# Global branch's output product: which groups stand between the last value product and the last attention outputs

## The chip, the cores and the metric

The kernel runs on one core of one Trainium2 chip. The metric is the device time of one execution in microseconds; before the change the median of three runs is 1576.53 us (1576.3 to 1577.41).

## The reference

One layer of a diffusion backbone over 1024 latent tokens of 1024 channels, with 256 context tokens that serve as further keys. Two attention branches run on the same input, A windowed and B global. What bears on the change is how their outputs are merged:

```python
def _global_attention(q, k_all, v_all):
    ...
        p = jax.nn.softmax(_gqa_scores(q_blk, k_all), axis=-1)
        return _gqa_values(p, v_all)
...
def _merge_branches(o_a, o_b, gate_logits, w_branch_a, w_branch_b, w_out):
    g_a, g_b = jnp.split(jax.nn.sigmoid(gate_logits), 2, axis=-1)
    return (g_a * (o_a @ w_branch_a) + g_b * (o_b @ w_branch_b)) @ w_out
...
        y = _latent_token_mixer(h, kv_ctx, w_in[l], b_in[l], attn_sink[l], q_norm_g[l], k_norm_g[l],
                                w_branch_a[l], w_branch_b[l], w_out[l], rope)
        x = _layer_norm(DEEPNORM_ALPHA * x + gate1 * y, ln1_g[l], ln1_b[l])
        h = x * (1.0 + scale2) + shift2
        y = _conv_ffn(h, w_up[l], conv_w[l], conv_b[l], w_down[l])
```

The change is in `o_b @ w_branch_b` times its gate: a product of 512 by 1024 weights with the outputs of the global branch.

## The kernel before, in words

Everything lies transposed: channels on the 128 partitions, tokens along the row. A tile of 128 channels by 1024 tokens is a feature tile, and there are eight of them, f = 0 to 7. A product in full precision is made of three matmuls on a high and a low part of each operand (`mm3`, lines 88 to 91): high by high (L89), low part of the outputs (L90), low part of the weights (L91). A high part is a rounded copy (L81 on ScalarE, L83 on GpSimd), a low part the difference (L86).

The attention runs in units of one branch, 128 query tokens and four heads. Line 831 loops over the units; each round merges three lists of steps by their place on a common scale and calls them: scores of the present unit, the value product of the unit before (transposes `ptr` of the probabilities, L530; their high and low parts `pth` and `ptl`, L539 and L540; the product `av`, L551 and L552), and filler steps. After the last unit (u == nu) only the value steps of the last unit and fillers are left. Its output goes through a copy `avs` on ScalarE (L557), `up` on GpSimd (L559), a sum `ot` on VectorE (L562), a scaling on GpSimd (L565) and the split into `O` on GpSimd (L83, L86). The output tiles `O` of the second token half (hf = 1) are complete only then; those of the first half (hf = 0) have been complete since the first four blocks of 128 tokens.

The fillers of the end belong to the output product of the global branch (br = 1). A group of `branch_steps` (line 802) is one feature tile and one token half: it loads the stored gate into `bT`, runs twelve matmuls into a bank `b`, and multiplies the bank into `bT` on VectorE (L813). `first` holds the groups of feature tiles 0 and 1 in the order (0, hf 0), (0, hf 1), (1, hf 0), (1, hf 1), on banks of the attention's pool `ps2`. Behind the attention a new pool of banks, `ps3`, is opened: `big` tiles of 1024 tokens, three of them, and `sml` tiles of 512, two of them. There `wb` (line 947) makes the high and low weights of tiles 2 to 5, `merge` (line 938) adds the two branches' products (L940) and splits the sum into `mh` (ScalarE) and `ml` (VectorE) for the output projection `y`, and the loop at line 953 takes tiles 2 to 7, both token halves alternating.

The kernel's scheduler decides where the instructions of a step stand on each engine's queue; each engine then takes its queue in order. SyncE issues most loads (`sgd` into `bT` at L955, weights at L901, `z` at L935), also in the order of its queue.

## Time and profile before

| | |
|---|---|
| median of three runs | 1576.53 us |
| the profiled execution | 1576.9 us, of which the span is 1575.1 |
| mean granted clock of TensorE | 0.995 |
| TensorE busy | 1526.1 us (97%) |
| VectorE busy | 1194.1 us (76%) |
| ScalarE busy | 808.9 us (51%) |
| GpSimd busy | 759.1 us (48%) |
| last value product ends, first output projection starts | 778.73 us, 821.77 us |

Times in the trace are microseconds from the start of the span. A matmul of 128 by 512 is shown with 0.39 us though the next one starts after 0.23: matmuls overlap, and the distance of their starts is what they cost. In the windows view the clock column is the share of full speed that TensorE was granted. In the timeline the bracket is the engine's idle time before the instruction and what ended it.

### The profile page before, as it was taken

To read this page: it belongs to the slowest core of one execution; us is meant where nothing else is said; L and a number is where in the kernel's file an instruction comes from. 1 tells how busy PE (TensorE), PEld (TensorE's weight loads), DVE (VectorE), ACT (ScalarE), POOL (GpSimd) and SP (SyncE) were. 2 spreads that over 40 slices of the span, in tenths; PEclk is the share of its full clock that TensorE was granted. 3 is DMA by queue.
4 is the path that set the end of the run, shared out by engine and by line. 5 is a ranking of instruction groups with operands and counts; after the bars stand their busy time and mean duration, and the time that the engine had idled before them with its cause. 6 is when DMAs were issued, how large, how long until landed. Compare 5 with 4: busy or idle time off the path is not lost.

```text
span 1575.1 us, 21929 instructions
## 1 busy us (share of the span) xinstructions
PE 1526.1 (97%) x7614; PEld 1264.2 (80%) x7614; DVE 1194.1 (76%) x1761; ACT 808.9 (51%) x1439; POOL 759.1 (48%) x737
## 2 busy tenths in 40 slices
PE   6999999999999999999999999999999999999997
PEld 5878788878886888777778898888888888888886
DVE  7797545728888777788684779888888888656797
ACT  5422222448888667688522465444544444435533
POOL 0574212426666566555422644666667765021053
PEclk9999999999999999999999999999999999999999
DMA  9685663322237565533354132333334446997823
GB/s 376 225 303 185 221 206 102 114 79 79 58 88 177 114 142 127 115 82 71 111 174 98 54 108 81 120 108 107 108 107 107 108 107 171 353 274 225 260 93 108
DMA packets 112016, 230.25 MB, mean 146 GB/s; under 512 B 13505, under 2 KB 27329, under 8 KB 111809
## 3 DMA queue, kind: packets, MB, share of 16 engines
q1 hardware_dynamic: 96464, 199.20, 38.5%
q0 software_dynamic: 10400, 20.19, 8.4%
q10 hardware_dynamic: 5040, 9.46, 1.6%
q8 instruction: 60, 0.98, 0.3%
q14 instruction: 52, 0.42, 0.1%
HBM read 177.61 MB, written 65.87 MB: 155 GB/s over the span
## 4 chain that ended last, share of the span: by engine, by line
PE 81%; DVE 8%; DMA 3%; ACT 3%; issue 3%; POOL 1%; SPq 0%; DVEq 0%; ACTq 0%; POOLq 0%
PE ptr L530 5%; PE p L90 4%; PE p L91 4%; PE p L89 4%; PE b L89 3%; PE b L90 3%; PE b L91 3%; PE g L89 3%; PE g L90 3%; PE g L91 3%; PE s L413 2%; PE av L551 2%; PE a L91 2%; PE c L89 2%; PE d L91 2%
## 5 line engine op out<-in xcount | busy, mean ns | idle before, releaser
L540 DVE TENSOR_TENSOR ptl<-ptr,pth 128x512 fp32r<-128x512 f32 x188 | 124.7, 684 | 28.2 <-ACT pth L539 25.5
L539 ACT CAST pth<-ptr 128x512 fp32r<-128x512 f32 x188 | 106.5, 588 | 59.1 <-PE ptr L530 35.5
L86 DVE TENSOR_TENSOR ld<-rd,hd 128x1024 fp32r<-128x1024 f32 x77 | 97.7, 1284 | 48.2 <-ACT hd L81 41.6
L530 PE MATMUL ptr<-ident,p 128*128 128x128 f32 x816 | 126.3, 277 | 7.4 <-DVE ptl L540 5.1
L425 ACT ACTIVATE p<-p,nm 128x1024 f32<-128x1024 f32 (+2 forms) x128 | 125.3, 981 | 10.7 <-DVE p L458 10.0
L530 PEld LDWEIGHTS ptr<-ident,p 128*128 128x128 f32 x816 | 93.9, 140 | 36.8 <-DVE ptl L540 10.9
L81 ACT CAST hd<-rd 128x1024 fp32r<-128x1024 f32 x77 | 79.6, 1051 | 85.3 <-PE p L91 61.4
L551 PE MATMUL av<-pth,VT 128*128 128x512 f32 x236 | 104.7, 444 | 1.0 <-ACT avs L557 0.5
L89 PE MATMUL p<-hd 128*128 128x512 f32 x264 | 103.2, 391 | 0.0
L91 PE MATMUL p<-hd,ld 128*128 128x512 f32 x264 | 102.7, 389 | 0.0
L90 PE MATMUL p<-ld,hd 128*128 128x512 f32 x264 | 102.7, 389 | 0.0
L86 POOL TENSOR_TENSOR wlg<-wg,whg 128x512 fp32r<-128x512 f32 x32 | 46.0, 1445 | 112.1 <-ACT whg L81 111.9
L89 PE MATMUL g<-hh,whg 128*128 128x512 f32 x256 | 99.9, 390 | 0.0
L91 PE MATMUL g<-hh,wlg 128*128 128x512 f32 x256 | 99.6, 389 | 0.0
L90 PE MATMUL g<-hl,whg 128*128 128x512 f32 x256 | 99.6, 389 | 0.0
L552 PE MATMUL av<-ptl,VT 128*128 128x512 f32 x236 | 97.6, 413 | 1.6 <-POOL ptl L86 1.4
L458 DVE TENSOR_SCALAR_CACHE_REDUCE p<-s,cvt,nmc 128x1024 f32<-128x1024 f32 x64 | 84.4, 1339 | 11.7 <-PE s L414 11.1
L413 PE MATMUL s<-KL,q 128*128 128x512 f32 (+2 forms) x192 | 76.0, 396 | 2.8 <-ACT p_x L425 2.0
L187 DVE CUSTOM_DVE_ANT_0 wml<-wml,sc,bmc 128x1024 f32<-128x1024 f32 x32 | 45.0, 1419 | 41.1 <-DMA wml<-in_wmodT_dram 40.3
L83 POOL TENSOR_SCALAR pth<-prw 128x512 fp32r<-128x512 f32 x48 | 31.2, 651 | 87.7 <-ACT prw L536 64.6
L81 ACT CAST wS<-s 128x512 fp32r<-128x512 f32 x76 | 45.3, 620 | 52.1 <-POOL s L1093 51.3
L414 PE MATMUL s<-KL,q 128*128 128x512 f32 (+2 forms) x192 | 71.7, 373 | 0.0
(402 smaller groups left out, 4943.3 us busy)
## 6 DMA issues: line engine op xcount, KB each, us to landing
wml<-in_wmodT_dram SPq DMA_DIRECT2D x48, 512.0 KB
ru<-in_w_up_dram SPq DMA_DIRECT2D x38, 512.0 KB
rd<-td SPq DMA_DIRECT2D x55, 256.0 KB
rd<-sd SPq DMA_DIRECT2D x44, 256.0 KB
rd<-in_w_dn_dram SPq DMA_DIRECT2D x33, 256.0 KB
wm<-in_wmodT_dram SPq DMA_DIRECT2D x16, 512.0 KB
wg<-in_w_g_dram SPq DMA_DIRECT2D x32, 256.0 KB
sgd<-sg ACTq DMA_DIRECT2D x32, 256.0 KB
```

Of the source, the lines that this page charges most:

```text
L81: cast[:] = [nc.scalar.copy(hi, src).ins]
L86: low[:] = [lo_eng.tensor_tensor(out=lo, in0=src, in1=hi.bitcast(F32), op=ALU.subtract).ins]
L89: nc.tensor.matmul(ps, a[0], b[0], start=start, stop=False, skip_group_check=resumed)
L90: nc.tensor.matmul(ps, a[0], b[1], start=False, stop=False, skip_group_check=resumed)
L91: nc.tensor.matmul(ps, a[1], b[0], start=False, stop=stop, skip_group_check=resumed)
L413: nc.tensor.matmul(o, self.q[0][:, hs], ks, start=True, stop=False)
L425: nc.scalar.activation(p, s, AF.Exp, bias=nm[:, h:h + 1], scale=scale, accum_out=sm[:, h:h + 1])
L530: nc.tensor.transpose(tr[:, h * P:(h + 1) * P], self.pslice(h, n), ident)
L539: nc.scalar.copy(hi, tr)
L540: nc.vector.tensor_tensor(out=lo, in0=tr, in1=hi.bitcast(F32), op=ALU.subtract)
L551: nc.tensor.matmul(self.av, v, hi, start=first, stop=False)
L552: nc.tensor.matmul(self.av, v, lo, start=False, stop=self.left == 0)
```

## The change

Of `first`, only the group (0, hf 0) stays among the value steps of the last unit. (1, hf 0) is called right behind the last value product. Then the new pool of banks is opened, and the first-half groups of feature tiles 2 and 3 are made on `big` tiles by a new function `half`. Only behind the last of their matmuls (`tc.issue_after`) come (0, hf 1) and (1, hf 1), which read the last outputs, now on `sml` tiles. The merges of tiles 0 and 1 follow, then the second halves of tiles 2 and 3, then both halves of tiles 4 to 7, one whole half after the other. The number of matmuls is the same.

```diff
@@ branch_steps
-                    steps.append(lambda f=f, hf=hf: grp(f, hf, pt_tile))
+                    steps.append(lambda mk=pt_tile, f=f, hf=hf: grp(f, hf, mk))
@@ the loop over the units
         if u == nu:
-            fs += first[0::2]
+            fs.append(first[0])
@@ behind the last value product
-    for st_ in first[1::2]:
-        st_()
-    hput("hwb1_0", "lwb1_0")
+    first[2]()
     ps2.release()
     att.release()
     qp.release()
@@ behind wb
+    pb = {}
+
+    def half(f, hf):
+        if f not in pb:
+            bT[1, f] = ht(f"bT1_{f}")
+            nc.sync.dma_start(bT[1, f], sgd[KT + f])
+            pb[f] = big(f"b1_{f}")
+        w = wb[f // 2]
+        for j in range(4):
+            k = (f % 2) * 4 + j
+            a = O[1, hf, 0, j // 2][:, j % 2], O[1, hf, 1, j // 2][:, j % 2]
+            i = mm3(pb[f][:, hsl(hf)], (w[0][:, k], w[1][:, k]), a, j == 0, j == 3)
+        return i
+
+    half(2, 0)
+    with tc.issue_after(half(3, 0)):
+        for n in (1, 3):
+            first[n](sml)
+    hput("hwb1_0", "lwb1_0")
     for f in (0, 1):
         merge(f)
     for f in range(2, KT):
-        bT[1, f] = ht(f"bT1_{f}")
-        nc.sync.dma_start(bT[1, f], sgd[KT + f])
-        w = wb[f // 2]
-        ps = big(f"b1_{f}")
-        for j in range(4):
-            k = (f % 2) * 4 + j
-            for hf in (0, 1):
-                a = O[1, hf, 0, j // 2][:, j % 2], O[1, hf, 1, j // 2][:, j % 2]
-                mm3(ps[:, hsl(hf)], (w[0][:, k], w[1][:, k]), a, j == 0, j == 3)
+        for hf in (0, 1):
+            if f > 3 or hf:
+                half(f, hf)
+        ps = pb[f]
         nc.vector.tensor_tensor(out=bT[1, f], in0=ps, in1=bT[1, f], op=ALU.mult)
         merge(f)
```

`mm3` now also returns its last matmul. Below, the order of instructions on an engine; the number behind a name is that of its buffer, and the lines of the changed kernel are shifted (merge at 938, the product of a whole tile at 975).

TensorE before, behind the last value product (`av1_7_1`): `b1_0_1` and `b1_1_1` are groups (0, hf 1) and (1, hf 1), `O1100` the older output tile of the second half, `O1101` and `O1111` the high and low part of the last outputs. Between the first and the second row stand the twelve matmuls on the older tiles, six for each group.

```order
L552 MATMUL av1_7_1_8659<-ptl1_7_1_9_8739,VT4_2104 128x512
L89 MATMUL b1_0_1_8765<-O1100_7435,hwb1_0_7973 128x512
...
L91 MATMUL b1_1_1_8780<-O1100_7435,lwb1_0_7974 128x512
L89 MATMUL b1_0_1_8765<-O1101_7648,hwb1_0_7973 128x512
L90 MATMUL b1_0_1_8765<-O1111_7649,hwb1_0_7973 128x512
...
L91 MATMUL b1_1_1_8780<-O1101_7648,lwb1_0_7974 128x512
L89 MATMUL b1_2_8826<-O1000_5477,hwb1_8806 128x512
```

TensorE in the changed kernel, at the same place: `b1_1_0` is group (1, hf 0), `hwb1`/`lwb1` the weights of tiles 2 and 3, `hwb2` those of tile 4.

```order
L552 MATMUL av1_7_1_8643<-ptl1_7_1_9_8723,VT4_2104 128x512
L89 MATMUL b1_1_0_8750<-O1000_5477,hwb1_0_7973 128x512
...
L90 MATMUL b1_2_8786<-O1010_5478,hwb1_8776 128x512
L89 MATMUL b1_3_8801<-O1000_5477,hwb1_8776 128x512
L90 MATMUL b1_3_8801<-O1010_5478,hwb1_8776 128x512
L89 MATMUL b1_4_8898<-O1000_5477,hwb2_8780 128x512
L91 MATMUL b1_2_8786<-O1000_5477,lwb1_8777 128x512
...
L89 MATMUL b1_0_1_8815<-O1100_7435,hwb1_0_7973 128x512
...
L89 MATMUL b1_0_1_8815<-O1101_7648,hwb1_0_7973 128x512
```

Before, 12 matmuls stand between the last value product and the first that reads the last outputs; now 43 do: 12 of `b1_1_0`, 5 that need only high weights of tiles 2 to 4, 20 more of tiles 2 and 3, and 6 of `b1_0_1` on the older outputs.

VectorE before, from the sum of the last outputs (`ot`) on:

```order
L562 TENSOR_TENSOR ot1_7_1_8756<-avs1_7_1_8752,up1_7_1_8754 64x256 x2
L86 TENSOR_TENSOR lwb1_8807<-rwb1_8575,hwb1_8806 128x1024
L813 TENSOR_TENSOR bT1_0_8611<-b1_0_1_8765,bT1_0_8611 128x512
L813 TENSOR_TENSOR bT1_1_8708<-b1_1_1_8780,bT1_1_8708 128x512
L86 TENSOR_TENSOR lwb2_8811<-rwb2_8577,hwb2_8810 128x1024
L940 TENSOR_TENSOR bT0_0_5492<-bT0_0_5492,bT1_0_8611 128x1024
L940 TENSOR_TENSOR bT0_1_5667<-bT0_1_5667,bT1_1_8708 128x1024
L86 TENSOR_TENSOR ml0_8816<-bT0_0_5492,mh0_8815 128x1024
L86 TENSOR_TENSOR ml1_8821<-bT0_1_5667,mh1_8820 128x1024
L963 TENSOR_TENSOR bT1_2_8824<-b1_2_8826,bT1_2_8824 128x1024
L940 TENSOR_TENSOR bT0_2_5914<-bT0_2_5914,bT1_2_8824 128x1024
L86 TENSOR_TENSOR lwo0_8965<-rwo0_8962,hwo0_8964 128x1024
```

VectorE in the changed kernel, from the same sum on (`lwo0` is the low part of the first weights of the output projection):

```order
L562 TENSOR_TENSOR ot1_7_1_8740<-avs1_7_1_8736,up1_7_1_8738 64x256 x2
L813 TENSOR_TENSOR bT1_1_8748<-b1_1_0_8750,bT1_1_8748 128x512
L86 TENSOR_TENSOR lwb1_8777<-rwb1_8575,hwb1_8776 128x1024
L86 TENSOR_TENSOR lwb2_8781<-rwb2_8577,hwb2_8780 128x1024
L86 TENSOR_TENSOR lwo0_8965<-rwo0_8962,hwo0_8964 128x1024
L813 TENSOR_TENSOR bT1_0_8646<-b1_0_1_8815,bT1_0_8646 128x512
L938 TENSOR_TENSOR bT0_0_5492<-bT0_0_5492,bT1_0_8646 128x1024
L813 TENSOR_TENSOR bT1_1_8748<-b1_1_1_8830,bT1_1_8748 128x512
L938 TENSOR_TENSOR bT0_1_5667<-bT0_1_5667,bT1_1_8748 128x1024
L86 TENSOR_TENSOR ml0_8846<-bT0_0_5492,mh0_8845 128x1024
L975 TENSOR_TENSOR bT1_2_8784<-b1_2_8786,bT1_2_8784 128x1024
L86 TENSOR_TENSOR ml1_8851<-bT0_1_5667,mh1_8850 128x1024
```

The product of group (1, hf 0), which stood among the value steps, is now ahead of `lwb1`; `lwo0` has moved ahead of both products of the last outputs and of the merges.

TensorE in the value stretch of the last unit, from the last matmul of the unit before (`av1_7_0`) on; `ptr1_7_1_2` is the third block of transposed probabilities. First before, then changed:

```order
L552 MATMUL av1_7_0_8480<-ptl1_7_0_9_8570,VT4_2104 128x512
L89 MATMUL b1_0_0_8613<-O1000_5477,hwb1_0_7973 128x512
L90 MATMUL b1_0_0_8613<-O1010_5478,hwb1_0_7973 128x512
...
L91 MATMUL b1_0_0_8613<-O1001_5737,lwb1_0_7974 128x512
L530 MATMUL ptr1_7_1_2_8627<-ident_58,p1_7_1_0_8429 128x128
```

```order
L552 MATMUL av1_7_0_8480<-ptl1_7_0_9_8570,VT4_2104 128x512
L530 MATMUL ptr1_7_1_2_8611<-ident_58,p1_7_1_0_8429 128x128
...
L530 MATMUL ptr1_7_1_3_8622<-ident_58,p1_7_1_3_8516 128x128
L89 MATMUL b1_0_0_8648<-O1000_5477,hwb1_0_7973 128x512
L90 MATMUL b1_0_0_8648<-O1010_5478,hwb1_0_7973 128x512
```

Group (0, hf 0) now stands behind two blocks of transposes instead of ahead of them.

More of the change, by code (lines that the diff above doesn't have):

```diff
@@ L90, in mm3 @@
         nc.tensor.matmul(ps, a[0], b[1], start=False, stop=False, skip_group_check=resumed)
-        nc.tensor.matmul(ps, a[1], b[0], start=False, stop=stop, skip_group_check=resumed)
+        return nc.tensor.matmul(ps, a[1], b[0], start=False, stop=stop, skip_group_check=resumed).ins
     const = ctx.enter_context(tc.tile_pool(name="const", bufs=1, side="left"))
```

## The prediction

> **What bounds the kernel now.** I began with the page: which engine is busy, and which share of the chain that ended last it carries.

> ```profile
> span 1575.1 us, 21929 instructions
> PE 1526.1 (97%) x7614; PEld 1264.2 (80%) x7614; DVE 1194.1 (76%) x1761; ACT 808.9 (51%) x1439; POOL 759.1 (48%) x737
> PE 81%; DVE 8%; DMA 3%; ACT 3%; issue 3%; POOL 1%; SPq 0%; DVEq 0%; ACTq 0%; POOLq 0%
> ```

> TensorE has work in 97% of the span, so a change of order can only win TensorE's gaps, and only those in the stretch that it touches. Second view: the table by stretches of 5 us around the last value product (columns: stretch, its length, busy time of PE, PEld, DVE, ACT and POOL with counts, granted clock, DMA share, GB/s), and one of its rows at half a microsecond.

> ```profile
> 780.00:785.00 5.00, 2.74 (x11) 1.72 (x10) 2.06 (x3) 1.24 (x2) 2.95 (x4) 1.00 0.95 370
> 785.00:790.00 5.00, 4.13 (x13) 2.84 (x12) 2.48 (x4) 0.00 (x0) 0.16 (x1) 0.66 1.01 394
> 785.50:786.00 0.50, 0.50 (x3) 0.40 (x2) 0.34 (x1) 0.00 (x0) 0.00 (x0) 0.50 1.02 410
> ```

> These ten microseconds hold the hole: TensorE idles 2.26 us in the first row, and in the second its granted clock is 0.66 on the mean, 0.50 where the last row looks. Third view: TensorE's timeline there (start, duration, operation; in brackets the idle time before it and what ended it).

> ```profile
> 778.56 0.39 PE L89 MATMUL b<-O,hwb 128*128 128x512 f32 x1
> ...
> 781.05 0.39 PE L91 MATMUL b<-O,lwb 128*128 128x512 f32 x1
> 783.39 0.50 PE L89 MATMUL b<-O,hwb 128*128 128x512 f32 x1 [1.95 <-POOL O L83]
> 784.20 0.50 PE L90 MATMUL b<-O,hwb 128*128 128x512 f32 x1 [0.30 <-POOL O L86]
> ...
> 785.46 0.59 PE L89 MATMUL b<-O,hwb 128*128 128x512 f32 x1
> ...
> 787.55 0.63 PE L91 MATMUL b<-O,lwb 128*128 128x512 f32 x1
> 789.05 0.47 PE L89 MATMUL b<-O,hwb 128*128 128x512 f32 x1 [0.87 <-DVE bT L813]
> ```

> Undisturbed matmuls follow each other at (781.05 - 778.56) / 11 = 0.227 us. After twelve of them TensorE waits for the last outputs, high part and then low part, and before the first group of feature tile 2 for the product (line 813) that reads a group's bank. What it waits for stands in the chain of waits:

> ```profile
> 778.49 0.24 PE av L552
> 778.75 0.60 ACT avs L557
> ...
> 780.59 0.43 DVE ot L562
> 781.14 1.71 POOL ot L565
> 782.93 0.41 POOL O L83
> 783.42 0.73 POOL O L86
> ```

> From the end of the last value product (778.73) to the low part of the last output (784.15) steps of ScalarE, GpSimd and VectorE take 5.4 us, whatever TensorE does.

> **The change, part by part.** I call V the moment after the last value product (778.56 in the trace).

> *The hole itself.* From 781.05 to 789.05 are 8.00 us, in which 13 matmuls start; at 0.227 us they need 2.95, so 5.05 us are lost: 2.1 for the high part (783.39 - 781.05 - 0.23), 0.6 for the low part, 1.2 in six matmuls at half clock (the first of them starts at 785.46, in the row of clock 0.50, the last at 787.55: 2.09 us for five steps that need 1.14, and the sixth is like them), 0.9 for line 813 and the rest at the edges. In the changed kernel 12 matmuls of (1, first token half), 24 of tiles 2 and 3 and one of tile 4 stand first, then 6 on the older outputs: 43 x 0.227 = 9.8 us before the high part is asked for, and the outputs are there at V + 5.6. Tile 2 has its own banks and waits for no line 813. I take +5.05, all of it. The half clock comes 2 us after a wait of 1.95 us and a second of 0.30; with those waits gone I let it go too. [...]

> *The value stretch.* Group (0, first half) moves behind two transposes' blocks, and group (1, first half) moves out to V.

> ```profile
> 763.59 0.50 PE L89 MATMUL b<-O,hwb 128*128 128x512 f32 x1
> 766.63 0.69 DVE L813 TENSOR_TENSOR bT<-b,bT 128x512 f32<-128x512 f32 x1 [2.52 <-PE b L91]
> 767.06 0.59 ACT L536 COPY prw<-ptr 128x512 f32<-128x512 f32 x1 [3.53 <-PE ptr L530]
> 771.92 0.66 PE L530 MATMUL ptr<-ident,p 128*128 128x128 f32 x4 [0.70 <-DVE ptl L540]
> ```

> Here VectorE idles 2.52 and ScalarE 3.53 us, because TensorE computes the group first and the transposes after; later TensorE waits 0.70 us for VectorE. With the transposes first both start nearly 12 x 0.227 = 2.7 us earlier, which pays for the 2.7 us of cover that go with the other group. Bounds: the whole 0.70 is won, or a second wait of that size arises. I take +0.5, nearer the win since both helpers have idle time at the start and the later wait is VectorE's alone.

> *A new wait, for the low half of the weights of tiles 2 and 3.* VectorE now stands at line 813 of (1, first half) until TensorE has done that group, and the subtraction that makes lwb, which before ran from 781.04, is queued behind it.

> ```profile
> 781.04 1.23 DVE L86 TENSOR_TENSOR lwb<-rwb,hwb 128x1024 fp32r<-128x1024 f32 x1
> 788.21 0.69 DVE L813 TENSOR_TENSOR bT<-b,bT 128x512 f32<-128x512 f32 x1 [1.87 <-PE b L91]
> 788.82 1.22 DVE L86 TENSOR_TENSOR lwb<-rwb,hwb 128x1024 fp32r<-128x1024 f32 x1
> 800.21 1.22 DVE L963 TENSOR_TENSOR bT<-b,bT 128x1024 f32<-128x1024 f32 x1
> 801.35 1.22 DVE L86 TENSOR_TENSOR lwb<-rwb,hwb 128x1024 fp32r<-128x1024 f32 x1
> ```

> Group ends at V + 2.72; line 813 starts 0.23 later (787.55 + 0.43 against 788.21), the next operation 0.61 after it (788.21 to 788.82), takes 1.23, and a matmul follows a VectorE result by 0.15 (788.90 to 789.05): V + 4.94. Until then TensorE has 12 + 5 matmuls, those that need only the high weights, to V + 3.86. So -1.1. It could be -0.7 if the starts lie closer, and -1.6 if the subtraction is slowed by GpSimd as below.

> *VectorE's backlog.* The first merges (line 940) wait for the groups of the last outputs, which now come 25 matmuls later, so VectorE, idle before, has to catch up by the time the output projection y starts. Operations of 1024 columns follow each other at 801.35 - 800.21 = 1.14 us.

> ```profile
> 811.41 1.21 DVE L963 TENSOR_TENSOR bT<-b,bT 128x1024 f32<-128x1024 f32 x1
> 816.53 1.22 DVE L963 TENSOR_TENSOR bT<-b,bT 128x1024 f32<-128x1024 f32 x1
> 821.97 1.23 DVE L963 TENSOR_TENSOR bT<-b,bT 128x1024 f32<-128x1024 f32 x1 [0.61 <-PE b L91]
> 826.53 0.39 PE L89 MATMUL y<-mh,hwo 128*128 128x512 f32 x1
> 827.03 0.50 PE L90 MATMUL y<-ml,hwo 128*128 128x512 f32 x1
> ```

> Let X be the end of the last group on the last outputs, (1, second half). Line 813 starts at X + 0.23 and takes 0.61; fourteen operations stand before the product of tile 5, which so starts at X + 0.84 + 14 x 1.14 = X + 16.8; two rounds of 5.12 us (811.41 to 816.53) bring that of tile 7 to X + 27.0. TensorE ends tile 7 after 119 matmuls, at X + 27.0, and the product can't start before X + 27.2. So VectorE has just caught up, with 0.2 us in hand, and the wait in y, 827.03 - 826.53 - 0.23 = 0.27 us, stays as it is. Whatever slows VectorE by more is paid in full. What could is GpSimd:

> ```profile
> L565 POOL TENSOR_TENSOR ot<-ot,rb x32: 722/731/1698, 368.5 to 781.1; 128x256 f32<-128x256 f32 x32
> 789.84 2.22 POOL L936 TENSOR_SCALAR z<-z 128x512 f32<-128x512 f32 x2 [5.70 <-DMA z<-in_xT_dram]
> 789.95 3.18 DVE L940 TENSOR_TENSOR bT<-bT,bT 128x1024 f32<-128x1024 f32 x2
> 795.16 26.55 SPq L935 DMA_DIRECT2D z<-in_xT_dram  x13
> ```

> GpSimd's product of 0.73 us took 1.70 beside lwb, and the two merges, 1.59 us each beside two z, lost 0.37 each. [...] A z meets some operation of each round before and after the change alike; only those in the first 17 us, where there is no longer any slack, count. Nothing is the least, five such meetings (2.0 us, rounded up from 1.85) the most, and I take -0.5, a little over one, since before the change VectorE still had to wait 0.61 us for tile 7 at the end.

> *Edits with nothing to them.* The loads of tiles 2 and 3 from line 955 go out earlier, behind the same work; the pool of banks is opened earlier; from tile 4 on TensorE's matmuls are as many as before, whole halves one after the other instead of alternating, at the same 0.227 us. The later program has the same order, and TensorE passes the shift on.

> Sum: 5.05 + 0.5 - 1.1 - 0.5 = 3.95 us. The profiled execution took 1576.9 us (span 1575.1), 0.37 over the median of 1576.53; 1576.9 - 3.95 = 1572.95, on the median 1572.6.

> **The rivals.**

> *The half clock stays.* Its 1.2 us are not won, or a stretch of 3.4 us at half clock follows the new 1.1 us wait, for 1.7: 1573.8 to 1574.3. For it: there is no row of a wait that shows what length is enough. Against it: the 0.70 us wait at 771 left the clock at full, and the new wait is nearer to that than to 1.95 + 0.30. Chance 0.13.

> *VectorE comes late to y.* The backlog is 2.0 us instead of 0.5, by the collisions with GpSimd: 1574.1. For it: no slack in the 17 us after X. Against: those two merges met two z back to back, while the other thirteen are issued over 26.55 us, so at most eight fall in those 17. Chance 0.17.

> *Slower: the weights of y hold VectorE.* lwo for tile 0 now stands on VectorE ahead of line 813 of (0, second half); before, it came after three merges. It needs ScalarE's hwo, and that a load, which SyncE issues now only after the last output's low part, at about V + 5.9.

> ```profile
> 784.56 0.89 SPq L935 DMA_DIRECT2D z<-in_xT_dram  x2
> 821.81 1.33 SPq L901 DMA_DIRECT2D rwo<-in_w_out_dram  x3
> 826.52 1.05 ACT L81 CAST hwo<-rwo 128x1024 fp32r<-128x1024 f32 x1 [0.98 <-DMA rwo<-in_w_out_dram]
> ```

> Landing took at most 5.3 us for a z (784.56 to 789.84) with the DMA engines full, and 4.7 for a rwo. So the load is there at V + 11.2, hwo at 12.3, lwo at 13.6. Line 813 of (0, second half) is wanted at V + 1.1 + 49 x 0.227 + 0.23 = 12.45 and thus 1.1 us late; with its merge it ends at 15.35, when that of (1, second half) is wanted at 15.2. So it costs 0.15 us. From there every microsecond of a later landing is one at y: it decides the sign from a landing over 9 us after issue, and at 12.8 us gives 7.5 us, 1580.1. For it: the DMA share is 0.95 and 1.01 in the two stretches at V. Against it: both landings measured. Chance 0.10.

> **How the numbers follow.** Forecast 0.60, half clock 0.13, VectorE late 0.17, held by the weights 0.10. A difference of 0.2%, 3.15 us, is about what a measurement of this kernel can tell from no change. Forecast alone lies between 1571.2 (no backlog, the wait at 0.7, the whole 0.70 won) and 1575.0; two rivals end inside. To hold 8 in 10 the range goes to 1576.0, which takes part of the loads that land a little late. Faster than 1573.4 is most of the forecast, 0.58; within, both middle rivals and the forecast's upper end, 0.31; slower 0.11.

> **What would show it.** In the new profile: after V no wait for O at lines 83 and 86; one wait of about 1.1 us for lwb on TensorE; granted clock 1.00 from 780 to 790; the wait of 0.70 in the value stretch smaller; the y matmul on ml7 waiting under 0.8 us. I am wrong if the clock falls again, if y waits for ml by 2 us, or if VectorE idles for the weights hwo ahead of line 813.

## The result, and the profile after

The changed kernel took 1574.19 us (median of 20 runs, 1571.62 to 1580.36), the kernel before 1578.65 us beside it (20 runs, 1575.34 to 1583.59): a ratio of 0.9973, 95% interval 0.9963 to 0.9983, or 2.7 to 5.8 us of 1576.5. The profiled execution took 1573.33 us, its span is 1571.6. 1572.6 was forecast, 3.95 us less than the median of three runs of before; taken off the 1578.65 of the 20 runs, 3.95 gives 1574.70.

Two executions of the same kernel don't reach the last value steps at the same time (line 497 of the kernel before stands at 762.97 in the first trace and at 766.30 in the second), so I compare a stretch inside the traces: from TensorE's transposition of the last sums (line 497) to the y matmul that needs ml7. It has three pieces: to the end of the last value product (V), from there to the first y matmul, and from the first to the 23rd y matmul, which is the one on ml7.

| kernel | to V | V to y | y to ml7 | sum |
|---|---|---|---|---|
| before, the trace of the prediction | 15.59 | 43.21 | 5.26 | 64.06 |
| before, a second trace (tenth experiment) | 15.63 | 42.04 | 5.08 | 62.75 |
| after the change | 11.69 | 42.02 | 5.90 | 59.61 |

Group (1, hf 0), twelve matmuls or 2.72 us, went from the first piece to the second. TensorE's timeline of the changed kernel:

```profile
764.55 0.27 PE L497 MATMUL str<-ident,sm 128*4 128x128 f32 x1
...
776.24 0.39 PE L89 MATMUL b<-O,hwb 128*128 128x512 f32 x1
...
779.64 0.39 PE L90 MATMUL b<-O,hwb 128*128 128x512 f32 x1
780.00 0.47 PE L89 MATMUL b<-O,hwb 128*128 128x512 f32 x1
781.18 0.50 PE L91 MATMUL b<-O,lwb 128*128 128x512 f32 x1 [0.71 <-DVE lwb L86]
...
824.16 0.50 PE L90 MATMUL y<-ml,hwo 128*128 128x512 f32 x1 [0.75 <-DVE ml L86]
```

The waits for O and for the bank are gone, and the 0.70 us wait among the value steps too. Left are two: lwb, 4.94 us after V as forecast (781.18 - 776.24), and ml7. In the windows (columns as before) the clock is whole:

```profile
780.00:785.00 5.00, 4.29 (x19) 3.32 (x19) 2.80 (x2) 0.00 (x0) 1.64 (x2) 1.00 0.46 165
785.00:790.00 5.00, 5.00 (x24) 4.14 (x23) 2.42 (x3) 1.05 (x1) 1.95 (x2) 1.00 0.95 360
```

The weights of y, named as what could turn the sign, came in time. ScalarE's cast and VectorE's next operations:

```profile
786.41 1.05 ACT L81 CAST hwo<-rwo 128x1024 fp32r<-128x1024 f32 x1 [7.49 <-DMA rwo<-in_w_out_dram]
787.50 1.23 DVE L86 TENSOR_TENSOR lwo<-rwo,hwo 128x1024 fp32r<-128x1024 f32 x1 [4.70 <-DMA z<-in_xT_dram]
788.77 0.69 DVE L813 TENSOR_TENSOR bT<-b,bT 128x512 f32<-128x512 f32 x1
```

lwo ends at 788.73; TensorE ends (0, hf 1) at 788.57, and its product starts the usual 0.2 us later, at 788.77: in time, and not 1.1 us late. Late VectorE is, but further on, where its operations meet GpSimd's scaling of z:

```profile
804.77 1.64 DVE L938 TENSOR_TENSOR bT<-bT,bT 128x1024 f32<-128x1024 f32 x1
806.33 1.63 DVE L86 TENSOR_TENSOR lwo<-rwo,hwo 128x1024 fp32r<-128x1024 f32 x1
807.88 1.63 DVE L86 TENSOR_TENSOR ml<-bT,mh 128x1024 fp32r<-128x1024 f32 x1
810.68 1.55 DVE L938 TENSOR_TENSOR bT<-bT,bT 128x1024 f32<-128x1024 f32 x1
```
```profile
804.22 2.67 POOL L934 TENSOR_SCALAR z<-z 128x512 f32<-128x512 f32 x2 [11.87 <-DMA z<-in_xT_dram]
807.70 3.46 POOL L934 TENSOR_SCALAR z<-z 128x512 f32<-128x512 f32 x4 [0.81 <-DMA z<-in_xT_dram]
```

### The profile page after: what moved, and what is told of

It reads as the page before. It is cut to its first block, busy times and chain, and to the rows that moved or that the text cites. A ratio compares the mean times of both kernels' runs of the same rounds, so it can differ in the third digit from the quotient of the medians.

```text
span 1571.6 us, 21932 instructions
## 1 busy us (share of the span) xinstructions
PE 1524.0 (97%) x7614; PEld 1264.4 (80%) x7614; DVE 1193.5 (76%) x1761; ACT 809.0 (51%) x1439; POOL 765.4 (49%) x737
## 5 line engine op out<-in xcount | busy, mean ns | idle before, releaser
L540 DVE TENSOR_TENSOR ptl<-ptr,pth 128x512 fp32r<-128x512 f32 x188 | 124.8, 685 | 29.1 <-ACT pth L539 27.7
L539 ACT CAST pth<-ptr 128x512 fp32r<-128x512 f32 x188 | 106.4, 588 | 58.2 <-PE ptr L530 34.2
L86 DVE TENSOR_TENSOR ld<-rd,hd 128x1024 fp32r<-128x1024 f32 x77 | 96.5, 1270 | 50.1 <-ACT hd L81 46.5
L530 PE MATMUL ptr<-ident,p 128*128 128x128 f32 x816 | 126.3, 278 | 7.9 <-DVE ptl L540 5.5
L81 ACT CAST hd<-rd 128x1024 fp32r<-128x1024 f32 x77 | 79.5, 1050 | 86.8 <-PE p L91 56.1
L530 PEld LDWEIGHTS ptr<-ident,p 128*128 128x128 f32 x816 | 93.7, 140 | 37.2 <-DVE ptl L540 11.2
L89 PE MATMUL p<-hd 128*128 128x512 f32 x264 | 103.2, 391 | 0.0
L91 PE MATMUL p<-hd,ld 128*128 128x512 f32 x264 | 102.7, 389 | 0.0
L90 PE MATMUL p<-ld,hd 128*128 128x512 f32 x264 | 102.7, 389 | 0.0
L89 PE MATMUL g<-hh,whg 128*128 128x512 f32 x256 | 99.9, 390 | 0.0
L86 POOL TENSOR_TENSOR wlg<-wg,whg 128x512 fp32r<-128x512 f32 x32 | 45.0, 1415 | 112.5 <-ACT whg L81 102.3
L91 PE MATMUL g<-hh,wlg 128*128 128x512 f32 x256 | 99.6, 389 | 0.0
L90 PE MATMUL g<-hl,whg 128*128 128x512 f32 x256 | 99.6, 389 | 0.0
L552 PE MATMUL av<-ptl,VT 128*128 128x512 f32 x236 | 97.5, 413 | 1.6 <-POOL ptl L86 1.4
L458 DVE TENSOR_SCALAR_CACHE_REDUCE p<-s,cvt,nmc 128x1024 f32<-128x1024 f32 x64 | 84.5, 1340 | 11.7 <-PE s L414 11.3
L83 POOL TENSOR_SCALAR pth<-prw 128x512 fp32r<-128x512 f32 x48 | 31.0, 646 | 87.3 <-ACT prw L536 63.8
L81 ACT CAST wS<-s 128x512 fp32r<-128x512 f32 x76 | 45.2, 620 | 51.0 <-POOL s L1105 50.2
```

What stands on the lines that cost most here:

```text
L81: cast[:] = [nc.scalar.copy(hi, src).ins]
L86: low[:] = [lo_eng.tensor_tensor(out=lo, in0=src, in1=hi.bitcast(F32), op=ALU.subtract).ins]
L89: nc.tensor.matmul(ps, a[0], b[0], start=start, stop=False, skip_group_check=resumed)
L90: nc.tensor.matmul(ps, a[0], b[1], start=False, stop=False, skip_group_check=resumed)
L91: return nc.tensor.matmul(ps, a[1], b[0], start=False, stop=stop, skip_group_check=resumed).ins
L458: nc.vector.tensor_scalar(out=p, in0=o, scalar1=self.qscale(nqs)[:, hs] if self.br else -1.0, scalar2=self.other[:, hs], op0=ALU.mult, op1 ...
```

## The experiments

All sums are of the stretch defined above.

**1. Half the cover.** Of tiles 2 and 3 only tile 2's first half stands in between.

```diff
-    half(2, 0)
-    with tc.issue_after(half(3, 0)):
+    with tc.issue_after(half(2, 0)):
...
```

> Only the first half of tile 2 stands between (1, first half) and the groups of the last outputs, not that of tile 3. I measure from the transposition of the last sums (line 497) to the y matmul that waits for ml7: 64.06 us before, 59.61 after the change. Theory: the cover is far longer than needed (43 matmuls, 9.8 us, against outputs ready 5.5 us behind the last value product); with 31 left there is still no wait for O, the wait for lwb stays at 1.1, and VectorE gets the groups of the last outputs 2.7 us earlier, so that the wait of 0.75 before the y matmul on ml7 falls to about 0.3: 59.1, the time about 0.5 us under the changed kernel. Rival: tile 3 is needed as cover; then a wait for O comes back and the stretch is 60.5 or more.

Measured: 11.68 + 42.02 + 6.29 = 59.99 us; ratio to before 0.9962 (0.9948 to 0.9976). No wait for O, and V to y as in the changed kernel: tile 3 was not needed as cover. But y waits no less for VectorE, though the groups of the last outputs came ten matmuls, 2.3 us, earlier:

```profile
825.14 0.50 PE L90 MATMUL y<-ml,hwo 128*128 128x512 f32 x1 [0.77 <-DVE ml L86]
```

So VectorE was not late at y because those groups come late.

**2. No cover by tiles 2 and 3.** Only the move of (1, hf 0) is left; the groups of the last outputs follow at once, on the old pool.

```diff
     first[2]()
+    for n in (1, 3):
+        first[n]()
...
-    half(2, 0)
-    with tc.issue_after(half(3, 0)):
-        for n in (1, 3):
-            first[n](sml)
...
```

> Tiles 2 and 3 stay where they were before; only (1, first half) is moved behind the last value product, and the groups of the last outputs follow it at once on banks of the old pool. Theory: moving one group gives most of the gain, since 18 to 24 matmuls are 4.1 to 5.5 us against outputs ready at 5.5; a wait of about 0.7 for the low part and one of 0.9 for the bank remain, the wait of 1.1 for lwb goes, and y waits 0.3 for ml7: 59.7 us from line 497 to y, time as the changed kernel. Rival: the cover by tiles 2 and 3 is what pays; then the hole with its half clock comes back and the stretch is 62.5 to 63.

Measured: 11.68 + 43.28 + 5.08 = 60.04 us; ratio 0.9969 (0.9960 to 0.9979). Two waits, no half clock, and y without a wait for VectorE:

```profile
781.64 0.50 PE L90 MATMUL b<-O,hwb 128*128 128x512 f32 x1 [1.04 <-POOL O L86]
786.67 0.47 PE L89 MATMUL b<-O,hwb 128*128 128x512 f32 x1 [0.88 <-DVE bT L813]
```

Against the first trace of before, moving one group brings 4.0 of the 4.45 us (against the second, which has no half clock, 2.7 of 3.1). Tiles 2 and 3 in between add 0.43, since they trade these waits for those for lwb and ml7.

**3. High weights first.** In the first halves of tiles 2 and 3 the matmuls on lwb stand last.

```diff
+            if late:
+                nc.tensor.matmul(ps, w[0][:, k], a[0], start=j == 0, stop=False)
+                nc.tensor.matmul(ps, w[0][:, k], a[1], start=False, stop=False)
...
+    half(3, 0)
+    lows(2)
+    with tc.issue_after(lows(3)):
```

> As the changed kernel, but in the first halves of tiles 2 and 3 the eight matmuls of each that need only high weights come first, those with the low weights behind. Theory: the wait for lwb (1.1 us) is the order of three matmuls and goes altogether, as 28 matmuls (6.4 us) need no lwb, which is ready at 4.9; VectorE has 0.64 us of slack ahead of the product of (1, second half), so about 0.45 us of it come back as a longer wait before y (1.2 instead of 0.75): 59.0 us. Rival 1: all of it comes back at y (1.8): 59.6. Rival 2: nothing comes back: 58.5.

Measured: 11.68 + 40.80 + 6.91 = 59.39 us; ratio 0.9971 (0.9962 to 0.9981). The wait for lwb is gone, 1.22 us, and 1.01 of it are back at y, now as two waits, the first because ScalarE gets its input late:

```profile
824.57 0.49 PE L89 MATMUL y<-mh,hwo 128*128 128x512 f32 x1 [0.55 <-ACT mh L81]
826.02 0.50 PE L90 MATMUL y<-ml,hwo 128*128 128x512 f32 x1 [0.95 <-DVE ml L86]
```

Nearest to the first rival: in this order VectorE, not TensorE, sets when y goes on.

**4. Tiles 2 and 3 in between, value steps as before.**

```diff
-            fs.append(first[0])
+            fs += first[0::2]
...
-    first[2]()
```

> Tiles 2 and 3 as in the changed kernel, but (0, first half) and (1, first half) stay among the value steps as before. It tells what the value stretch gained by itself. Theory: the value stretch takes 15.6 us again instead of 11.7 plus the 2.7 of the group that moved out, so 1.2 us are lost there; TensorE has only two matmuls before it needs lwb, ready 3.9 us behind the last value product, and waits about 3.4 us in one piece; in all 63.1 us from line 497 to y without a half clock, up to 1.7 more with one. Rival: the gain in the value stretch is chance of that execution; then 62 or less, with the stretch at 14.4.

Measured: 15.63 + 44.23 + 6.11 = 65.97 us; ratio 1.0012 (0.9998 to 1.0026). The value stretch is back at its old length, so its gain is no chance. The waits behind it were two, since ScalarE's hwb was late as well, and the half clock held for 6.8 us, twice as long as in the first trace of before:

```profile
782.28 0.50 PE L89 MATMUL b<-O,hwb 128*128 128x512 f32 x1 [1.62 <-ACT hwb L81]
784.25 0.80 PE L91 MATMUL b<-O,lwb 128*128 128x512 f32 x1 [1.24 <-DVE lwb L86]
```

Tiles 2 and 3 alone thus bring nothing: without (1, hf 0) ahead of them they are wanted before their weights are split.

**5. Sixes first.** As the second, but on the new pool's small tiles, and both groups' six matmuls on the older outputs stand ahead of their six on the last ones.

```diff
...
+    for js in (range(2), range(2, 4)):
+        for n in (1, 3):
+            first[n](sml, js)
...
```

> Tiles 2 and 3 back in their old place (as in the second experiment), the groups of the last outputs on the new pool's small tiles, and both groups' six matmuls on the older outputs ahead of their six on the last ones. Measure as before: line 497 to the y matmul on ml7 (64.06 before, 59.61 changed, 60.04 second experiment). Theory: 24 matmuls (5.45 us) cover the outputs, ready at 5.5, so the waits of 1.04 for O and 0.88 for the bank go and no wait for lwb comes; VectorE is 1.1 us closer to TensorE at the end, so y waits about 0.5 for ml7: 58.1 us. Rival: VectorE's chain sets the end whatever TensorE does; then all 2.4 us come back before y and the stretch is 59.5 or more.

Measured: 11.67 + 40.80 + 5.53 = 58.00 us; ratio 0.9967 (0.9955 to 0.9979). As forecast: no wait between V and y, where 180 matmuls at 0.227 are 40.9, and one short one at ml7. TensorE is busy throughout:

```profile
774.00:779.00 5.00, 5.00 (x24) 4.14 (x23) 2.75 (x5) 2.48 (x3) 2.69 (x4) 1.00 0.71 250
779.00:784.00 5.00, 5.00 (x24) 4.09 (x23) 4.49 (x6) 0.84 (x1) 0.65 (x1) 1.00 0.98 360
```

It is 1.6 us better than the change in this stretch, 0.1% of the kernel; the intervals of whole runs can't tell the two apart.

**6. Both groups out of the value steps.** Tiles 2 and 3 stay in their old place; the groups of the last outputs are on the small tiles.

```diff
-            fs.append(first[0])
...
+    first[0]()
     first[2]()
...
```

> Both first-half groups of tiles 0 and 1 leave the value steps and stand behind the last value product; tiles 2 and 3 stay in their old place. It tells what a group among the value steps covers. Theory: transposes and value products alone need 8.9 us on TensorE from line 497 to the end of the last value product if nothing waits, but ScalarE's and VectorE's copies of ten blocks don't keep up and about 1.5 us of waits appear (10.4 us); behind it 30 matmuls (6.8 us) cover the outputs: 59.6 us in all. Rival 1: a group among the value steps is no cover at all: 58.2. Rival 2: it is fully cover (2.7 us lost): 60.9.

Measured: 10.80 + 43.52 + 5.10 = 59.42 us; ratio 0.9972 (0.9959 to 0.9984). Without any group the value steps need 11.69 - 2.72 = 8.97 us of matmuls, if the changed kernel waits nowhere there (its timeline shows no wait), and 1.8 are lost in waits:

```profile
769.48 0.66 PE L530 MATMUL ptr<-ident,p 128*128 128x128 f32 x4 [0.70 <-DVE ptl L540]
772.83 0.50 PE L552 MATMUL av<-ptl,VT 128*128 128x512 f32 x1 [0.43 <-POOL ptl L86]
```

Before the change, with two groups of 2.72 us, 15.6 - 5.44 - 8.97 = 1.2 were lost; with one group behind two blocks of transposes, none. The place of a group counts for more than the number of them.

**7. z on ScalarE.**

```diff
-            nc.gpsimd.tensor_scalar(out=z, in0=z, scalar1=ALPHA, scalar2=0.0, op0=ALU.mult, op1=ALU.add)
+            nc.scalar.mul(z, z, ALPHA)
```

> The changed kernel with the scaling of z (line 934) on ScalarE instead of GpSimd, nothing else. Theory (collision): the wait of 0.75 before the y matmul on ml7 is 4 to 5 VectorE operations with two inputs in SBUF that took 1.55 to 1.64 us instead of 1.22 beside a z; without GpSimd they take 1.22, and y waits 0.3 or less: 59.1 us from line 497. Rival 1 (length): VectorE's list itself is too long; the wait stays at 0.7. Rival 2: ScalarE, held by a z that has not landed, brings mh late; y waits over 1 us.

Measured: 11.69 + 42.03 + 7.35 = 61.07 us; ratio 0.9966 (0.9954 to 0.9979). The second rival: every VectorE operation now took 1.22 to 1.23 us, but ScalarE stood at a z that had not landed, with mh queued behind it:

```profile
823.45 0.63 ACT L934 ACTIVATE z<-z 128x512 f32<-128x512 f32 x1 [1.80 <-DMA z<-in_xT_dram]
823.99 1.03 ACT L81 CAST mh<-bT 128x1024 fp32r<-128x1024 f32 x1
```

So this run shows that the operations are short without GpSimd, but not what y would gain by it. Behind the stretch, from 827.3, the clock was half for 3.4 us. The whole run is not slower: 1.5 us are within what its interval leaves open.

**8. z not scaled at all.** The line is left out; the residual enters the layer norm without its factor.

> The changed kernel with the scaling of z (line 934, GpSimd) left out: the residual enters the first layer norm without its factor. So neither GpSimd meets VectorE nor does ScalarE wait for a z. Theory (collision): every VectorE operation of 1024 columns from 789 on takes 1.2 us, the product of tile 7 waits for TensorE and not for VectorE, and the wait before the y matmul on ml7 falls from 0.75 to 0.3: 59.1 us from line 497. Rival (length): VectorE's list is too long even so; the wait stays at 0.6 to 0.8.

Measured, in one run: 11.69 + 42.03 + 5.08 = 58.80 us. VectorE's operations are short, and for the product of tile 7 it waits for TensorE:

```profile
804.97 1.22 DVE L937 TENSOR_TENSOR bT<-bT,bT 128x1024 f32<-128x1024 f32 x1
...
818.66 1.23 DVE L974 TENSOR_TENSOR bT<-b,bT 128x1024 f32<-128x1024 f32 x1 [0.50 <-PE b L91]
```

With that the excess at y is shown, in this one trace, to be the collision with GpSimd: 0.82 us, 5.90 against 5.08, which is also what the second trace of before has.

**9. One long wait.** The second experiment, with the matmul on the low part of the last outputs first.

```diff
+                if late:
+                    nc.tensor.matmul(ps, wh[:, k], a[1], start=n == 0, stop=False)
+                    nc.tensor.matmul(ps, wh[:, k], a[0], start=False, stop=False)
+                    nc.tensor.matmul(ps, wl[:, k], a[0], start=False, stop=n == 3)
```

> As the second experiment (tiles 2 and 3 in their old place), but the groups of the last outputs begin with the matmul on the low part of the last outputs, so TensorE has only the 12 matmuls of (1, first half) and then one single wait of 2.3 to 2.6 us. It asks what idle time costs the clock. By the traces so far (half clock after 1.95 + 0.30 and after 1.62 + 1.24, none after 1.04 or 0.71): half clock for 3.4 us, up to 15 matmuls at 0.43 us instead of 0.23. [...]

Measured, in one run: 11.68 + 44.83 + 5.42 = 61.93 us. The wait, and the two microseconds that begin 0.2 behind its end:

```profile
783.29 0.50 PE L815 MATMUL b<-O,hwb 128*128 128x512 f32 x1 [2.63 <-POOL O L86]
```
```profile
783.50:785.50 2.00, 2.00 (x10) 1.62 (x10) 0.82 (x1) 0.00 (x0) 0.00 (x0) 1.00 1.02 418
```

No half clock, against the expectation drawn from the traces so far: a longer wait than those of the kernel before left the clock whole here. A half clock stands in this trace at 873.7, behind the stretch.

**10 and 11. The kernel before, and the ninth, once more.** Nothing is edited. They ask whether the half clock goes with the pattern of the waits, so that it comes in each execution or in none, or also with their position, the place in time at which they come.

> The kernel before, unchanged, profiled once more. Its first trace shows half clock for 3.4 us after waits of 1.95 and 0.30; the ninth experiment shows none after 2.63. [...] Rival (pattern): two waits close together cause it; then it is there again at the same place, 64.1.

> The ninth experiment once more: 12 matmuls of (1, first half), then one wait of about 2.6 us. Theory (position): a half clock may follow this time, 63.1 to 63.6 us from line 497 instead of 61.9. Rival (pattern): never after a single wait of this length, 61.9 again.

Measured: before 62.75 us, the ninth 64.00 us. Both turned round. In the kernel before the same two waits are there, without a half clock (one stands at 874.2 instead, behind the stretch):

```profile
786.76 0.51 PE L89 MATMUL b<-O,hwb 128*128 128x512 f32 x1 [1.95 <-POOL O L83]
787.57 0.50 PE L90 MATMUL b<-O,hwb 128*128 128x512 f32 x1 [0.30 <-POOL O L86]
```
```profile
788.00:790.00 2.00, 2.00 (x11) 1.60 (x9) 0.69 (x1) 0.00 (x0) 0.00 (x0) 1.00 1.03 412
```

and in the ninth the same single wait, with one:

```profile
781.30 0.50 PE L815 MATMUL b<-O,hwb 128*128 128x512 f32 x1 [2.63 <-POOL O L86]
```
```profile
783.00:785.00 2.00, 2.00 (x7) 1.52 (x6) 0.00 (x0) 0.00 (x0) 0.00 (x0) 0.50 1.02 411
```

So the pattern of the waits alone does not decide it. Where in time the half clocks of these traces begin is worked out at the end of this document.

## Why the prediction was right

The sign, the range and the mechanism held, and the forecast of 3.95 us lies within 2.7 to 5.8. That it came so close is partly luck, since two terms were off in opposite directions: the value stretch was put 0.7 us too low, and the hole up to 1.2 us too high. In the traces the gain is 4.45 us against the first one of before and 3.14 against the second. Term by term:

| term | forecast | measured | from |
|---|---|---|---|
| the hole | +5.05 | +5.05, or +3.88 where before has no half clock | 43.21 against 42.04 from V to y in the two traces of before |
| the value stretch | +0.5 | +1.2 | 15.59 and 15.63 against 11.69 + 2.72 |
| the wait for lwb | -1.1 | -1.1 to -1.2 | 1.08 by the starts of the matmuls; experiment 3 without it: 1.22 less from V to y |
| VectorE late at y | -0.5 | -0.64 and -0.82 | 5.26 and 5.08 against 5.90 |

*The hole.* Its waits went as worked out, but 1.2 us of it were the half clock, and I took for fixed what changes from one execution to the next: of two traces of the kernel before one has it. More than two executions speak on this: the mean granted clock is on record for each run, 0.9948 on the mean of the 52 runs of before beside experiments 1 to 7 and 0.9962 on that of the 20 of the change (the seven variants, all but the fourth, have 0.9959 to 0.9967 on the same measure). The difference, 0.0014 of 1576 us, is at most 2.2 us of gain by the clock, anywhere in the program. So the change does win clock on the average; how much of that lies in the hole is not shown.

*The value stretch* was sized too small. I asked only what would become of the 0.70 us wait. Experiment 4 gives the old length again with the old places, and experiments 2 and 6 bound it: one group behind the second pair of blocks hides all, two in the old places leave 1.2 us of waits, none leaves 1.8. Of the 1.2, 0.7 is the wait that the timeline names; the rest is in small pieces that no row names, so of what they are made stays open.

*The wait for lwb* came out to about a tenth: 17 matmuls, then 1.08 us (781.18 - 779.64 - 2 x 0.227). *VectorE late* was the right mechanism, collisions with GpSimd, and about the right size. Experiment 8 shows it; experiment 7 shows only that the operations are short without GpSimd, and experiment 1 that earlier groups of the last outputs do not cure it. In the prediction's sum this term stood for about one collision; the changed kernel has four, each 0.3 to 0.4 us long, of which part was hidden. The weights that could hold VectorE cost nothing: ScalarE began on them 4.3 us after the load's issue (782.12 to 786.41), where 5.3 had been reckoned with. The landing of 12.8 us, by which that rival was priced at 1580.1, no run shows.

What I did not see is that these terms belong to different halves of the change. Moving (1, hf 0) made nearly all of the gain by itself (experiment 2); the first halves of tiles 2 and 3 are not needed as cover, cost the wait for lwb and push VectorE into the z, and win only 0.4 us more. Six matmuls of each group on older outputs, in the right place, do the same without those costs (experiment 5).

Open is by how much whole runs differ between these versions: all but the fourth lie at 0.996 to 0.997 of before, with intervals of 0.001 to 0.0014 to either side.

## What to carry to other kernels

Before new work is put into a hole, count what is enough: here the outputs come 5.5 us after the last value product and 24 matmuls that need nothing new were there already, so 43 bought waits elsewhere. Where a filler hides little (here ahead of the transposes), moving it can win time by itself: 1.2 us here. A half clock seen in one trace should be counted with a chance, not as a sure gain, until a second trace shows it.

## What the runs showed of the hardware

A wait of 2.63 us was followed by half clock in one execution and not in the other, and so were waits of 1.95 and 0.30. What the traces have in common is the distance between the starts of their half clocks. In steps of 0.1 us, the half clock begins at 99.4 and 785.5 in the first trace of before, and at 100.0 and 782.7 in the eleventh experiment; those are 686.1 and 682.7 us apart, 201 and 200 times 3.413, and these four stretches lasted 3.4 us or twice that. In the changed kernel it begins at 100.7 and 1565.0, 1464.3 us or 429 times 3.413 apart, in the tenth experiment at 99.4 and 874.2, 774.8 us or 227 times. The 3.413 us is worked out from these starts and lengths: between 3.39 and 3.43 no other step fits all four distances to 0.1 us.

So I cut each trace into windows of 3.413 us, counted from one of its half clocks. The window before the half clock was idle for 1.6 us of 3.4 in before (782.07 to 785.48) and for 2.0 in the eleventh (779.3 to 782.7). In the ninth and tenth the worst window of the stretch was idle for 1.8 and 1.6, and none followed. So idle time alone draws no sharp line in this range.

```profile
870.82:874.23 3.41, 3.24 (x23) 2.71 (x22) 1.59 (x2) 0.00 (x0) 1.00 (x1) 1.00 0.00 0
874.23:877.64 3.41, 3.41 (x9) 2.63 (x9) 1.81 (x6) 0.00 (x0) 1.03 (x1) 0.50 0.00 0
```

In the changed kernel from 804 to 813, a VectorE operation with two inputs in SBUF took 1.55 to 1.64 us beside a GpSimd scaling of z (804.77 to 810.68), and 1.22 to 1.23 without one (803.64 and 813.40); the product at line 975, with one input in a bank, took 1.22 ahead of the scalings (802.50) and 1.21 beside one (809.43).
